# Rotation tables of a state space mixer: two groups side by side in the partitions, laid out for each group by SBUF transfers

## The chip, the cores and the metric

The kernel runs on one core of a Trainium2 chip. The metric is the device time of one execution in microseconds. A core has five engines with instruction streams of their own: TensorE (PE in the rows), VectorE (DVE), ScalarE (ACT), GpSimd (POOL) and SyncE (SP), which in this kernel issues the transfers (DMA). Each engine works through its stream strictly in order, so an instruction that waits holds up all that stand behind it.

## The reference

One decoder layer with two mixers side by side. A normalised input is projected to q, k, v and u. Windowed attention runs over q, k, v; u goes through a diagonal complex state space model with 32 channel groups of 16 channels and 64 states each.

```python
def ssm_mixer(u, h0_re, h0_im, a_re, a_im, log_dt, b_re, b_im, c_re, c_im, d_skip, w_glu, b_glu):
    lr, li, bbr, bbi = zoh_discretize(a_re, a_im, log_dt, b_re, b_im)
    xr = jnp.einsum('blgh,gph->blgp', uf, bbr)
    xi = jnp.einsum('blgh,gph->blgp', uf, bbi)
    ...
    _, _, hr, hi = lax.associative_scan(_ssm_combine, (ar, ai, xr, xi), axis=1)
    y = (jnp.einsum('blgp,ghp->blgh', hr, c_re.astype(f32))
         - jnp.einsum('blgp,ghp->blgh', hi, c_im.astype(f32))
         + d_skip.astype(f32) * uf)
    g = jax.nn.gelu(y)
    ...
```

Each state is multiplied by the same complex number lambda = |lambda| e^(i theta) at every step. Behind the mixers come an output projection with a residual and a SwiGLU feed-forward network. All of it is float32.

## The kernel before

The program has stages: the projection to u together with the parameters of the state space model (`phase_u`, `phase_prep`, about the first 133 us), the mixers (`phase_mix`, to about 556 us), the output projection and the feed-forward network (to the end).

**The state space model.** 2064 prompt tokens are taken in 258 chunks of 8 (`NPC`; with the sample tokens 266, `NC`). For each group TensorE makes the chunk's input to the state, `px <- u, mi`. VectorE turns it into a rotating frame: `xt` and `xs` are `px` times cosine and sine of the angle 8 c theta of chunk c. In that frame the recurrence is real, so one scan on VectorE (`gg`) runs over all chunks. VectorE turns the result back (`xt`, `xs` again, then `hc`), and TensorE makes the outputs `yp <- u, it` and adds `yp <- hc, mo` in the same bank. A group's 64 states fill the 128 partitions twice: real parts in one half, imaginary parts in the other. The rotation of a state's two halves is by the same angle.

**The tables.** `co` and `si` hold these cosines and sines for four groups at a time, as tiles of 128 x 4 x 258, for m = 0 to 7. `ssm_tab1` computes on VectorE the angles in turns, reduced to half a turn on either side: `y` is the angle rounded to whole turns (a multiplication by `ph` and the addition of MAGIC), `f` what is left, from `phh` and `phl`, the angle of 8 theta in two parts. `ssm_tab2` makes the sines on ScalarE: `si` from f, with a scale of either sign in the two halves of the partitions (`s2p`), and `co` from the absolute value of f. As both halves of the partitions have the same angle, each is computed twice. `f` and `y` have one buffer (pool `m_f`), `co` and `si` two (`m_cs`).

**The order of the work.** No instruction is issued where the code stands. All calls go to a `Plan`, which notes them with the tiles that they read and write, and then issues them in the order of a list schedule: of the instructions whose inputs are ready by its own estimates, the one with the longest remaining path goes first. So an edit in one place can move instructions of other stages. All instructions of a trace carry the line of the helper that issues them (L263 before, L279 after); they are told apart by their tiles. The mixers' work is noted by `mix_step`, which interleaves attention tiles with the model's groups; `tab(...)` in it notes the pieces of `ssm_tab1` of a later m.

**Names in the rows.** `pu` are the products of the projection to u, `us` that result in SBUF, `uD` its place in DRAM, from which `u` is read back, laid out for the chunks. `pa` are the products of the projection to q, k, v; `qn` is q normalised, `pt` its transposition on TensorE, `qT` and `kT` the transposed q and k, `ps` the scores, `P` the softmax. `mo`, `t1` are the output matrices of four groups, `mi`, `it`, `gl` matrices that are loaded. The trace's rows leave out all numbers in names, so that `t1` is `t` there.

Of the kernel before, what the change touches and what calls it, by code (L numbers as in the profile page):

```python
# [8 lines left out]
F32 = mybir.dt.float32  # L9
# [8 lines left out]
NP_ = 2064            # prompt tokens with the meta tokens  # L18
TOK = 2128            # and the sample tokens
NT = 17  # L20
NC = TOK // 8         # chunks of 8 tokens
NPC = NP_ // 8
T0 = 16               # the meta tokens go no further than the mixers
TC, TS = 352, 704     # tokens of a chunk and of a block of the last phases
# [5 lines left out]
# columns of the constant array  # L30
# [26 lines left out]
class Lazy:  # L57
    """a view of a tile that is yet to be allocated"""
# [29 lines left out]
    def region(self):  # L88
        return {0} if self.base.psum else set(np.unique(self.idx[::self.base.step]).tolist())
# [80 lines left out]
class Plan:  # L170
    """Stands in for nc: notes the instructions, then issues them in the order of a list schedule
    (longest remaining path first) that keeps every dependency."""
# [9 lines left out]
    def dram(self, shape, dtype, name, blocks):  # L182
        """a scratch array; dependencies are kept by the numbers of its blocks"""
        t = LazyTile(self.bank, [1, 1], dtype, {"name": name})
        t.got, t.psum, t.step = self.dp.tile(list(shape), dtype, name=name), False, 1
        t.count = 1
        return Lazy(t, np.broadcast_to(blocks, shape), (), dtype)

    def turn(self, old, *new):
        """pools that take the place of old ones, once all that was noted on those is through"""  # L190
# [27 lines left out]
    def note(self, eng, name, args, kw):  # L218
# [10 lines left out]
        for t, r, w in use:  # L229
# [11 lines left out]
            for n, rr in t.writes + (t.reads if w else []):  # L241
                if n not in deps and not rr.isdisjoint(r):
                    deps.add(n)
        for t, r, w in use:
            t.first = o.n if t.first is None else t.first
            (t.writes if w else t.reads).append((o.n, r))
            t.pool.ops.add(o.n)
# [41 lines left out]
    def ported(self, eng, name, outs, args, kw):  # L289
        """whether it uses the pair of ports to SBUF that VectorE and GpSimd share"""  # L290
# [9 lines left out]
    def price(self, eng, name, args, kw):  # L300
        """nanoseconds on its engine, and until what follows a transfer may start"""
# [23 lines left out]
    def issue(self):  # L325
# [14 lines left out]
        # a bank is given out once all that its matrix products read has been scheduled  # L340
# [12 lines left out]
        # one that an engine writes for products to be added to it takes a bank that the last product wrote all of  # L353
# [59 lines left out]
class K:  # L413
# [9 lines left out]
    def split_w(self, h, l, raw, g):  # L423
        """h + l = g * raw, both parts exact in float32r"""
# [15 lines left out]
    # ------------------------------------------------------------------ set up  # L440
# [41 lines left out]
    # ------------------------------------------------------------------ u = rms(x) W_u  # L482
    def phase_u(self):
# [12 lines left out]
        for b, n in enumerate((384, 384, 384, 384, 256, 336)):  # L496
# [26 lines left out]
            # 1 / rms of the tokens, in both orientations  # L523
# [26 lines left out]
    # ------------------------------------------------------------------ S5 parameters  # L550
    def phase_prep(self):
# [18 lines left out]
        self.ph, self.phh, self.phl = (pp.tile([128, 32], F32, name=n) for n in ("ph", "phh", "phl"))  # L570
# [4 lines left out]
        self.s2p = pp.tile([128, 1], F32, name="s2p")  # L575
        nc.vector.tensor_scalar(self.s2p, self.sg, TWO_PI, None, op0=ALU.mult)
# [4 lines left out]
        if True:  # L581
# [48 lines left out]
            # theta / 2 pi in turns, as a sum of two floats  # L630
# [19 lines left out]
            nc.vector.tensor_add(self.ph, b8, e8)  # L650
            e8 = add(sub(b8, self.ph), e8)
            hh = cut(self.ph)
            nc.vector.tensor_copy(self.phh, hh)
            nc.vector.tensor_add(self.phl, sub(self.ph, hh), e8)
            # lambda^n, n = 0..8
# [22 lines left out]
            # f = (lambda - 1) / Lambda  # L678
# [20 lines left out]
            # lambda^8 h0  # L699
# [5 lines left out]
            # zero rows of the Toeplitz scratch  # L705
# [3 lines left out]
            # E[(ri p), g, j, h] = lambda^(7-j) B: the taps and, transposed, the chunk input map  # L709
            Ks = t32(shape=(128, 32, 16))  # L710
            # lambda^(7-j)
# [32 lines left out]
    # ------------------------------------------------------------------ S5 mixer  # L744
# [5 lines left out]
    def ssm_mats(self, m):  # L750
        """inputs and matrices of the four groups 4m.."""
# [37 lines left out]
    def ssm_tab1(self, m, piece):  # L789
        """rotations by multiples of 8 theta: the angles in turns"""  # L790
        nc, tp = self.nc, self.m_t
        ix = self.cst[:, C_IX:C_IX + NPC]
        if piece == 0:
            self.m_f = [self.m_fp.tile([128, 4, NPC], F32, name=nm) for nm in "fy"]
        f, y = self.m_f
        if piece == 0:
            for g in range(4):
                nc.vector.tensor_scalar(y[:, g], ix, self.ph[:, 4 * m + g:4 * m + g + 1], MAGIC,
# [3 lines left out]
        elif piece < 6:  # L802
            g = piece - 2
            q = slice(4 * m + g, 4 * m + g + 1)
            nc.vector.scalar_tensor_tensor(f[:, g], ix, self.phh[:, q], y[:, g], op0=ALU.mult, op1=ALU.subtract)
            nc.vector.scalar_tensor_tensor(f[:, g], ix, self.phl[:, q], f[:, g], op0=ALU.mult, op1=ALU.add)
# [4 lines left out]
    def ssm_tab2(self, m):  # L811
        nc, (f, y) = self.nc, self.m_f
        co, si = self.m_st[m][5:7]
        nc.scalar.activation(si, f, AF.Sin, scale=self.s2p)
        nc.scalar.activation(f, f, AF.Abs)
        nc.scalar.activation(co, f, AF.Sin, scale=-TWO_PI, bias=self.hp2)
# [940 lines left out]
```

## Time and profile before

| what | us |
|---|---|
| time, median of three runs | 2153.76 |
| lowest and highest | 2153.35, 2155.02 |
| span of the profiled execution | 2151.2 |
| TensorE busy | 2092.8 (97% of the span) |
| VectorE busy | 1730.0 (80%) |
| ScalarE busy | 1361.0 (63%) |
| GpSimd busy | 88.5 (4%) |

The profile is of one execution, whose span is from the first to the last instruction. Busy time is summed for each engine by itself; an engine that is not busy may be waiting or have nothing to do. The granted clock (PEclk) is TensorE's, as a share of its full speed.

### The profile page before, as it was taken

The page shows a single profiled execution, that of the slowest core. Times are in us where ns is not written, and L with a number is a line of the kernel's source. Part 1 is how long each engine was busy: PE and PEld are TensorE (multiplying, and loading weights), DVE is VectorE, ACT ScalarE, POOL GpSimd, SP SyncE. Part 2 cuts the span into 40 slices and gives each one's busy share as a digit, 9 for nine tenths or more (in the row PEclk, how much of TensorE's full clock was granted, in tenths as well). Part 3 has the DMA queues.
Part 4 walks back from the last instruction along what each step waited for, and adds up shares of the span by engine and source line. Part 5 has one row for each costly group of instructions (what it writes and reads, how often), then busy time and mean ns, then how long its engine had stood idle before and what let it go on. Part 6 is the DMA issues. An engine that isn't in the chain of part 4 may idle for free.

```text
span 2151.2 us, 35211 instructions
## 1 busy us (share of the span) xinstructions
PE 2092.8 (97%) x12557; PEld 1969.8 (92%) x12557; DVE 1730.0 (80%) x3773; ACT 1361.0 (63%) x3001; POOL 88.5 (4%) x80
## 2 busy tenths in 40 slices
PE   7999999999999999999999999999999999999998
PEld 7987777776898999999999999999999999999998
DVE  8889899875488769888787898877878987877876
ACT  6437888878544437566566757656656775665665
POOL 2011011101011000000000000000000000000000
PEclk9999999999899999999999999999999999999999
DMA  6682232214343545323322543332323722222222
GB/s 225 168 171 63 67 94 75 64 53 122 96 122 98 179 152 175 103 74 106 106 79 79 174 160 112 106 98 84 109 69 103 242 83 89 79 69 87 80 71 87
DMA packets 195152, 235.06 MB, mean 109 GB/s; under 512 B 54000, under 2 KB 155792, under 8 KB 194832
## 3 DMA queue, kind: packets, MB, share of 16 engines
q1 hardware_dynamic: 194976, 232.81, 35.4%
q8 instruction: 99, 1.62, 0.3%
q14 instruction: 77, 0.63, 0.1%
HBM read 187.92 MB, written 45.83 MB: 109 GB/s over the span
## 4 chain that ended last, share of the span: by engine, by line
PE 87%; DVE 8%; ACT 2%; DMA 2%; issue 1%; POOL 0%; DVEq 0%; ACTq 0%; POOLq 0%; SPq 0%
PE ga L263 24%; PE gc L263 12%; PE db L263 11%; PE da L263 8%; PE po L263 7%; PE pa L263 6%; PE gb L263 6%; PE ps L263 6%; PE pu L263 2%; PE pt L263 2%; PE px L263 1%; PE yp L263 1%; ACT wb L263 1%; DVE xs L263 1%; DVE acc L263 1%
## 5 line engine op out<-in xcount | busy, mean ns | idle before, releaser
L263 PE MATMUL ga<-X,wb 128*128 128x352 f32 x3168 | 723.2, 324 | 7.0 <-ACT acc L263 2.9
L263 PEld LDWEIGHTS ga<-X,wb 128*128 128x128 f32 x3168 | 544.7, 188 | 10.8 <-ACT gb L263 3.8
L263 PE MATMUL gc<-X,wb 128*128 128x352 f32 x1584 | 403.4, 324 | 1.4 <-ACT acc L263 1.4
L263 ACT ACTIVATE wb<-S 128x512 fp32r<-128x512 f32 (+1 forms) x306 | 187.5, 617 | 155.2 <-PE ga L263 74.6
L263 PEld LDWEIGHTS gc<-X,wb 128*128 128x128 f32 x1584 | 279.6, 188 | 2.1 <-ACT acc L263 2.0
L263 DVE TENSOR_TENSOR wb<-S,wb 128x512 fp32r<-128x512 f32 (+1 forms) x306 | 203.8, 672 | 57.5 <-ACT wb L263 26.9
L263 ACT ACTIVATE wb<-r 128x512 fp32r<-128x512 f32 (+1 forms) x242 | 146.9, 613 | 127.2 <-PE gc L263 47.5
L263 PE MATMUL gb<-X,wb 128*128 128x352 f32 x792 | 217.5, 323 | 0.0
L263 PE MATMUL da<-wb 128*128 128x352 f32 x936 | 208.9, 323 | 3.2 <-DVE acc L263 1.6
L263 DVE TENSOR_TENSOR wb<-r,wb 128x512 fp32r<-128x512 f32 (+1 forms) x242 | 160.2, 670 | 54.8 <-PE gb L263 24.2
L263 PE MATMUL db<-wb 128*128 128x352 f32 x792 | 162.9, 323 | 4.5 <-ACT db L263 4.5
L263 PEld LDWEIGHTS da<-wb 128*128 128x128 f32 x936 | 159.6, 188 | 5.3 <-ACT wb L263 4.6
L263 ACT ACTIVATE wb<-fr 128x512 fp32r<-128x512 f32 (+1 forms) x166 | 101.9, 619 | 93.7 <-PE gc L263 40.7
L263 PE MATMUL db<-gb,wb 128*128 128x352 f32 x792 | 161.1, 323 | 0.0
L263 PE MATMUL pa<-wb,xh 128*128 128x512 f32 (+3 forms) x544 | 156.2, 372 | 0.0
L263 DVE TENSOR_TENSOR wb<-fr,wb 128x512 fp32r<-128x512 f32 (+1 forms) x166 | 111.0, 675 | 41.0 <-PE gb L263 16.9
L263 PEld LDWEIGHTS gb<-X,wb 128*128 128x128 f32 x792 | 142.6, 188 | 0.0
L263 PEld LDWEIGHTS db<-wb 128*128 128x128 f32 x792 | 132.8, 188 | 6.0 <-ACT db L263 6.0
L263 PEld LDWEIGHTS db<-gb,wb 128*128 128x128 f32 x792 | 133.0, 188 | 0.3 <-ACT db L263 0.3
L263 ACT ACTIVATE acc<-db 128x352 f32<-128x352 f32 x288 | 119.4, 457 | 20.6 <-PE db L263 19.9
L263 PE MATMUL po<-oh,wb 128*128 128x352 f32 x576 | 121.3, 334 | 1.8 <-ACT oh L263 1.1
L263 ACT ACTIVATE db<-acc 128x352 f32<-128x352 f32 x276 | 120.4, 465 | 2.4 <-DVE ru L263 2.2
(252 smaller groups left out, 3885.8 us busy)
## 6 DMA issues: line engine op xcount, KB each, us to landing
r<-w_up SPq DMA_DIRECT2D x41, 512.0 KB
r<-w_gate SPq DMA_DIRECT2D x38, 512.0 KB
r<-w_down SPq DMA_DIRECT2D x34, 512.0 KB
fr<-w_gate SPq DMA_DIRECT2D x28, 512.0 KB
fr<-w_down SPq DMA_DIRECT2D x26, 512.0 KB
fr<-w_up SPq DMA_DIRECT2D x25, 512.0 KB
acc<-xT SPq DMA_DIRECT2D x6, 1408.0 KB
hD<-acc SPq DMA_DIRECT2D x6, 1408.0 KB
```

The source lines that it names most:

```text
L263: getattr(getattr(self.nc, eng), name)(*[f(v) for v in args], **{k: f(v) for k, v in kw.items()})
```

## The change

`phase_prep` now lays out the angles for two groups side by side: the even group of a pair in the first 64 partitions, the odd one in the other 64, so that `ph`, `phh`, `phl` have 16 columns in place of 32. `ssm_tab1` computes `f` and `y` as 128 x 2 x 258. `ssm_tab2` makes on ScalarE the sine with both signs (`sp`, `sn`), the absolute value and the cosine (into `y`), all 128 x 2 x 258. Then eight transfers for each m, each from one half of the partitions to a half of `si` or `co`, give every group its table in both halves. They are issued by SP, with the other transfers. `sp` and `sn` are in the pool of `f` and `y`, with one buffer. `mix_step` notes fewer pieces. The rest of the diff changes how `Plan` keeps track of dependencies (sets of numbers become bit masks, and entries that a later write covers are dropped), and takes comments out.

```diff
@@ phase_prep
-        self.ph, self.phh, self.phl = (pp.tile([128, 32], F32, name=n) for n in ("ph", "phh", "phl"))
+        self.ph, self.phh, self.phl = (pp.tile([128, 16], F32, name=n) for n in ("ph", "phh", "phl"))
...
-        self.s2p = pp.tile([128, 1], F32, name="s2p")
-        nc.vector.tensor_scalar(self.s2p, self.sg, TWO_PI, None, op0=ALU.mult)
...
-            nc.vector.tensor_add(self.ph, b8, e8)
-            e8 = add(sub(b8, self.ph), e8)
-            hh = cut(self.ph)
-            nc.vector.tensor_copy(self.phh, hh)
-            nc.vector.tensor_add(self.phl, sub(self.ph, hh), e8)
+            ph = add(b8, e8)
+            e8 = add(sub(b8, ph), e8)
+            hh = cut(ph)
+            pl = add(sub(ph, hh), e8)
+            for y, x in ((self.ph, ph), (self.phh, hh), (self.phl, pl)):
+                for a in range(2):
+                    r = slice(64 * a, 64 * a + 64)
+                    nc.vector.tensor_copy(y[r], x[r].rearrange("p (g a) -> p g a", a=2)[:, :, a])
@@ ssm_tab1
-            self.m_f = [self.m_fp.tile([128, 4, NPC], F32, name=nm) for nm in "fy"]
-        f, y = self.m_f
+            self.m_f = [self.m_fp.tile([128, 2, NPC], F32, name=nm) for nm in ("f", "y", "sp", "sn")]
+        f, y = self.m_f[:2]
         if piece == 0:
-            for g in range(4):
-                nc.vector.tensor_scalar(y[:, g], ix, self.ph[:, 4 * m + g:4 * m + g + 1], MAGIC,
+            for e in range(2):
+                nc.vector.tensor_scalar(y[:, e], ix, self.ph[:, 2 * m + e:2 * m + e + 1], MAGIC,
                                         op0=ALU.mult, op1=ALU.add)
...
-        elif piece < 6:
-            g = piece - 2
-            q = slice(4 * m + g, 4 * m + g + 1)
-            nc.vector.scalar_tensor_tensor(f[:, g], ix, self.phh[:, q], y[:, g], op0=ALU.mult, op1=ALU.subtract)
-            nc.vector.scalar_tensor_tensor(f[:, g], ix, self.phl[:, q], f[:, g], op0=ALU.mult, op1=ALU.add)
+        elif piece < 4:
+            e = piece - 2
+            q = slice(2 * m + e, 2 * m + e + 1)
+            nc.vector.scalar_tensor_tensor(f[:, e], ix, self.phh[:, q], y[:, e], op0=ALU.mult, op1=ALU.subtract)
+            nc.vector.scalar_tensor_tensor(f[:, e], ix, self.phl[:, q], f[:, e], op0=ALU.mult, op1=ALU.add)
@@ ssm_tab2
-        nc, (f, y) = self.nc, self.m_f
+        nc, (f, y, sp, sn) = self.nc, self.m_f
         co, si = self.m_st[m][5:7]
-        nc.scalar.activation(si, f, AF.Sin, scale=self.s2p)
+        nc.scalar.activation(sp, f, AF.Sin, scale=TWO_PI)
+        nc.scalar.activation(sn, f, AF.Sin, scale=-TWO_PI)
         nc.scalar.activation(f, f, AF.Abs)
-        nc.scalar.activation(co, f, AF.Sin, scale=-TWO_PI, bias=self.hp2)
+        nc.scalar.activation(y, f, AF.Sin, scale=-TWO_PI, bias=self.hp2)
+        for out, parts in ((si, (sn, sp)), (co, (y, y))):
+            o = out.rearrange("p (e a) c -> p e a c", a=2)
+            for d in range(2):
+                for a in range(2):
+                    nc.sync.dma_start(o[64 * d:64 * d + 64, :, a], parts[d][64 * a:64 * a + 64])
@@ mix_step
-        tab(2)
+        tab(2, 3)
...
-        tab(3)
...
-        tab(5, 6)
```

The order changes on every engine from the projection to u to the first part of the output projection; the feed-forward network's order is the same. Three places follow, all in the mixer's opening. The numbers behind the names tell buffers apart.

SP, the transfers from the last part of `us` to the first tables' matrices; first before, then after:

```order
L263 DMA uD_75<-us_1393 1024x1x74
L263 DMA r_1472<-xT 128x8x128
L263 DMA r_1491<-xT 128x8x128
L263 DMA uD_75<-us_1393 1024x1x74 x3
L263 DMA mi_1627<-miD_78 128x4x128
L263 DMA u_1639<-uD_75 128x1x266 x2
L263 DMA it_1655<-kD_77 16x4x128 x4
```

```order
L279 DMA uD_75<-us_1393 1024x1x74
L279 DMA si_1536<-sn_1512 64x2x258 x2
L279 DMA uD_75<-us_1393 1024x1x74 x3
L279 DMA co_1579<-y_1437 64x2x258
L279 DMA si_1536<-sp_1506 64x2x258 x2
L279 DMA mi_1621<-miD_78 128x4x128
L279 DMA u_1633<-uD_75 128x1x266 x2
L279 DMA co_1579<-y_1437 64x2x258 x3
L279 DMA it_1661<-kD_77 16x4x128 x4
```


Two `si` transfers now stand ahead of the last three `uD`, and three more ahead of `mi` and `u`; the last three of `co` come behind `u`.

TensorE, from the last `pa` of one attention tile on; before, then after:

```order
L263 MATMUL pa_1665<-wb_449,xl_1466 128x256
L263 MATMUL pt_1759<-idt_199,qn_1752 128x128 x4
L263 MATMUL pa_1769<-wb_449,xh_1602 128x512 x2
L263 MATMUL pa_1769<-wb_449,xl_1681 128x512
...
L263 MATMUL pa_1769<-wb_449,xh_1602 128x512
L263 MATMUL yp_1785<-u_1639,it_1655 128x266
L263 MATMUL yp_1789<-u_1639,it_1655 128x266
L263 MATMUL yp_1785<-hc_1625,mo_1653 128x266
...
L263 MATMUL pt_1798<-idt_199,qn_1752 128x128
```

```order
L279 MATMUL pa_1655<-wb_447,xl_1478 128x256
L279 MATMUL yp_1740<-u_1633,it_1661 128x266
...
L279 MATMUL yp_1740<-hc_1610,mo_1626 128x266
...
L279 MATMUL pt_1775<-idt_199,qn_1768 128x128 x4
L279 MATMUL pa_1786<-wb_447,xh_1629 128x512 x2
L279 MATMUL pa_1786<-wb_447,xl_1651 128x512
...
L279 MATMUL pt_1808<-idt_199,qn_1768 128x128
```


`yp` came behind `pt` and seven `pa` of the next tile; now it comes ahead of both, directly behind the last `pa` of the tile before.

VectorE, the way from `t1` to `hc` of the first two groups; before, then after:

```order
L263 TENSOR_TENSOR f_1563<-f_1563,y_1537 128x1032
L263 TENSOR_TENSOR t1_1642<-ls_114,c2_298 128x512
L263 TENSOR_TENSOR mo_1653<-lr_112,c1_253 128x512
...
L263 TENSOR_TENSOR xl_1681<-r_1414,xh_1602 128x1024
L263 TENSOR_TENSOR xt_1697<-px_1678,co_1552 128x258
...
L263 TENSOR_TENSOR xt_1697<-xt_1697,xs_1703 128x516
...
L263 SCALAR_TENSOR_TENSOR gg_1742<-mag8_1138,xt_1697 128x258 x2
L263 TENSOR_TENSOR qn_1752<-pa_1522,s_1662 128x512
L263 TENSOR_TENSOR xt_1697<-gg_1742,co_1552 128x516
...
L263 TENSOR_TENSOR qn_1752<-pa_1549,s_1662 128x128
L263 TENSOR_TENSOR hc_1625<-xt_1697,xs_1703 128x2x257
```

```order
L279 TENSOR_TENSOR t1_1614<-ls_114,c2_298 128x512
...
L279 TENSOR_TENSOR xl_1651<-r_1416,xh_1629 128x1024
L279 TENSOR_TENSOR mo_1666<-lr_112,c1_253 128x512
L279 TENSOR_TENSOR t1_1676<-ls_114,c2_298 128x512
L279 TENSOR_TENSOR xs_1681<-px_1668,si_1536 64x258
...
L279 TENSOR_TENSOR xt_1686<-xt_1686,xs_1681 128x516
L279 TENSOR_SCALAR y_1721<-cst_203,ph_1074 128x258
L279 SCALAR_TENSOR_TENSOR gg_1725<-mag8_1086,xt_1686 128x258 x2
L279 TENSOR_SCALAR y_1721<-cst_203,ph_1074 128x258
...
L279 TENSOR_TENSOR hc_1610<-xt_1686,xs_1681 128x2x257
L279 TENSOR_SCALAR y_1721<-y_1721 128x516
L279 TENSOR_TENSOR qn_1768<-pa_1528,s_1635 128x512
```


Before, the first row is the end of table m=1 (after, the rows begin at `t1`). Now a second `mo` and `t1` stand ahead of the first `xs`, two `y` of table m=1 stand inside the chain, the rest of that table comes behind `hc`, and `qn` has gone from ahead of `hc` to behind it.

## Rows read from the trace of the kernel before

**Rows 1.** The page: the span, and the busy time of the engines

```profile
span 2151.2 us, 35211 instructions
...
PE 2092.8 (97%) x12557; PEld 1969.8 (92%) x12557; DVE 1730.0 (80%) x3773; ACT 1361.0 (63%) x3001; POOL 88.5 (4%) x80
```

**Rows 2.** By stretch: length, busy PE, PEld, DVE, ACT, POOL, granted clock, DMA share, GB/s

```profile
175.00:500.00 325.00, 322.59 (x1663) 239.19 (x1662) 274.44 (x855) 260.10 (x642) 34.73 (x39) 1.00 0.26 73
```

**Rows 3.** Timeline of TensorE, the mixer's opening: start, length, work, [idle before, releaser]

```profile
153.77 1.12 PE L263 MATMUL pt<-idt,qn 128*128 128x128 f32 x4 [2.21 <-DVE qn L263]
...
157.41 1.06 PE L263 MATMUL yp<-u,it 128*128 128x266 f32 x4
...
158.30 1.06 PE L263 MATMUL yp<-hc,mo 128*128 128x266 f32 x4
```

**Rows 4.** Busy time by stretch: the opening's wait, and what follows it

```profile
150.40:153.80 3.40, 1.19 (x9) 0.90 (x8) 3.36 (x10) 1.97 (x4) 0.00 (x0) 0.98 0.60 166
...
153.80:157.20 3.40, 3.40 (x11) 2.88 (x12) 3.34 (x6) 0.69 (x1) 0.00 (x0) 0.52 0.65 177
```

**Rows 5.** Timeline of TensorE: two waits elsewhere

```profile
53.32 0.43 PE L263 MATMUL pb<-idt,rx 128*128 128x128 f32 x2 [1.69 <-POOL rx L263]
...
547.38 2.80 PE L263 MATMUL pt<-idt,P 16*128 16x16 f32 x12 [3.42 <-ACT P L263]
```

**Rows 6.** Busy time by stretch: behind those waits

```profile
54.60:61.60 7.00, 6.24 (x22) 5.75 (x22) 6.59 (x11) 1.81 (x3) 0.00 (x0) 0.51 0.68 179
...
546.10:559.90 13.80, 12.26 (x56) 11.03 (x57) 9.24 (x22) 11.77 (x33) 0.00 (x0) 0.51 0.05 17
```

**Rows 7.** Groups by line: busy us, mean ns of one, idle before

```profile
L263 DVE TENSOR_SCALAR y<-cst,ph 128x258 f32<-128x258 f32 x32 | 9.9, 349 | 0.3 <-DMA kD<-t 0.3
...
L263 DVE SCALAR_TENSOR_TENSOR f<-cst,phl,f 128x258 f32<-128x258 f32 x32 | 14.4, 480 | 0.0
...
L263 DVE TENSOR_SCALAR y<-y 128x1032 f32<-128x1032 f32 x8 | 5.5, 692 | 0.0
...
L263 DVE TENSOR_TENSOR f<-f,y 128x1032 f32<-128x1032 f32 x8 | 9.8, 1228 | 0.1
...
L263 ACT ACTIVATE si<-f,s2p 128x1032 f32<-128x1032 f32 x8 | 9.3, 1158 | 7.4 <-DVE f L263 7.3
...
L263 ACT ACT_TABLE_LOAD x26 | 33.4, 1283 | 1.2 <-PEq L1747 0.7
```

**Rows 8.** ScalarE around its table load: timeline, then a stretch's busy time

```profile
160.07 1.28 ACT L263 ACT_TABLE_LOAD   x1
...
161.36 0.74 ACT L263 ACTIVATE sq<-sq 128x266 f32<-128x266 f32 x2
...
168.44 0.40 ACT L263 ACTIVATE P<-P,nm 128x128 f32<-128x128 f32 x1 [1.10 <-DVE nm L263]
...
161.40:168.40 7.00, 7.00 (x40) 5.59 (x39) 6.29 (x25) 2.53 (x6) 1.41 (x1) 1.00 0.24 69
```

**Rows 9.** Timeline of VectorE, the mixer's opening

```profile
144.51 0.69 DVE L263 TENSOR_TENSOR t<-ls,c 128x512 f32<-128x512 f32 x1 [1.69 <-DMA uD<-us]
...
145.12 0.69 DVE L263 TENSOR_TENSOR mo<-lr,c 128x512 f32<-128x512 f32 x1
...
148.33 0.41 DVE L263 TENSOR_TENSOR xt<-px,co 128x258 f32<-128x258 f32 x1
...
153.05 0.66 DVE L263 TENSOR_TENSOR qn<-pa,s 128x512 f32<-128x512 f32 x1
...
155.97 0.68 DVE L263 TENSOR_TENSOR hc<-xt,xs 128x514 f32<-128x514 f32 x1
```

**Rows 10.** The chain that ended last: start, length, what

```profile
113.30 6.17 DMA r<-xT
...
135.82 8.50 DMA uD<-us
```

**Rows 11.** Timeline of SP's transfer issues, the mixer's opening

```profile
137.89 1.63 SPq L263 DMA_DIRECT2D u<-uD  x2
```

More of the change, by code (lines that the diff above doesn't have):

```diff
@@ L88, in region @@
     def region(self):
-        return {0} if self.base.psum else set(np.unique(self.idx[::self.base.step]).tolist())
+        if self.base.psum:
+            return 1
+        i = self.idx[::self.base.step]
+        i = i[tuple(slice(0, 1) if s == 0 else slice(None) for s in i.strides)].ravel()
+        bits = np.zeros(int(i.max()) + 1, bool)
+        bits[i] = True
+        return int.from_bytes(np.packbits(bits, bitorder="little").tobytes(), "little")
 def _rearrange(x, pat, n):
@@ L240, in note @@
                 order.add(t.first)
-            for n, rr in t.writes + (t.reads if w else []):
-                if n not in deps and not rr.isdisjoint(r):
+            for n, rr in t.writes:
+                if rr & r:
                     deps.add(n)
+            if w:
+                for n, rr in t.reads:
+                    if rr & r:
+                        deps.add(n)
         for t, r, w in use:
             t.first = o.n if t.first is None else t.first
-            (t.writes if w else t.reads).append((o.n, r))
+            if w:
+                t.writes = [(n, rr) for n, rr in t.writes if rr & ~r]
+                t.reads = [(n, rr) for n, rr in t.reads if rr & ~r]
+                t.writes.append((o.n, r))
+            else:
+                t.reads.append((o.n, r))
             t.pool.ops.add(o.n)
```

## The prediction

> **What bounds the kernel now.** I read the page first: the span is 2151.2 us, and TensorE is busy for 2092.8 us of it, 97% [rows 1]. VectorE comes second with 1730.0 us. The change edits work of VectorE, ScalarE and the transfer queue, all of it in the mixer (about 133 to 556 us), so busy shares over the whole span decide nothing; the next view is the busy time by stretch. From 175 to 500 us TensorE is busy 322.59 of 325.00 us at a granted clock of 1.00, while VectorE has 274.44 [rows 2]. VectorE is heavily used there, but TensorE waits only 2.41 us in all. Whatever VectorE is relieved of in this stretch can return 2.41 us and no more.
>
> The timeline of TensorE then shows where the mixer does wait. One place is its opening: the pa products (the projection to q, k and v) run out and TensorE stands for 2.21 us, from 151.56 until qn comes from VectorE at 153.77 [rows 3]. In the stretch after that wait the granted clock is 0.52, that is the lower of its two levels, with TensorE busy for all 3.40 us [rows 4]. The other is at the mixer's end: 3.42 us for P, a softmax on ScalarE [rows 5], with a clock of 0.51 from 546.1 to 559.9 us behind it [rows 6].
>
> **VectorE's saving.** Per table m (there are eight) the kernel before runs four y<-cst (349 ns), eight multiply-adds (480 ns, as in the row on phl; the four on phh are like it), two passes of 692 ns over 1032 elements and one of 1228 ns [rows 7]. Their busy time is 1.40 + 3.84 + 1.38 + 1.23 = 7.85 us. After, there are two and four of the narrow ones and the wide ones have 516 elements. Halving the last three by width (a lower bound, each has a fixed part) gives 0.70 + 1.92 + 0.69 + 0.61 = 3.92 us. So VectorE is spared some 3.9 us per table, 31 us in all. Nearly all of it lies under a TensorE that does not wait. I take half of the 2.41 us back: **-1.2 us**, bounds -2.4 and 0.
>
> **ScalarE.** Three passes of about 1.1 us (the sine row: 1158 ns [rows 7]) become four over half as many elements: between half the price each (2.3 us) and my value of 0.65 us each, 2.6 us, so the engine is spared under 1 us per table. But the sine needs another function table than tanh and exp, and ScalarE's new order puts six table loads around table m=1, where there was one; in the whole program 30 instead of 26. A load takes 1283 ns [rows 7]. The one in that stretch before starts at 160.07 and the next activation at 161.36 [rows 8], so nothing is added to it. Ahead of the first exp of P, 168.44 before, come four of the loads and two of the sines: 5.1 + 1.3 = 6.4 us of ScalarE. From 161.4 to 168.4 us it was busy for 2.53 of 7.00 us [rows 8], so it has 4.5 us free and the exp could be some 1.9 us late; pt<-P of TensorE comes behind it, with products of the next tile to fill the time. I take **+0.5 us**, bounds 0 and 3.
>
> The Trainium skill, page "ScalarE: Activation LUTs", section "What ACT_TABLE_LOAD costs", gives the same 1283 ns for the load and adds a drain of about 1380 ns to each switch. The row shows no such gap after the load, so here I go by the row. By the page the four loads would cost 10.7 us and not 5.1 us.
>
> **The opening, where the sum is decided.** Before, both first tables are done on VectorE before the stretch begins to press. VectorE then waits until 144.51 for the last uD<-us transfer (the u projection's result on its way to DRAM, whose buffer t1 takes over) [rows 9]; the chain gives that transfer 8.50 us from 135.82 [rows 10]. From there VectorE runs without a gap: t1, mo, the norm, xl, xt at 148.33, qn at 153.05, hc at 155.97 [rows 9]. In the changed order three things move.
>
> First, SP issues two of the new si transfers (132 KB each) ahead of the last three uD<-us. 264 KB at the 166 to 177 GB/s of this stretch [rows 4] are 1.5 us. The transfers may also share the engines and delay nothing, so the bounds are 0 and 1.6. I take 1.5: the chain shows that uD is what VectorE waits for. Five new transfers go ahead of mi and u, of which px is made; an SP issue there takes 0.6 to 0.8 us (two u in 1.63) [rows 11], so u is 3 to 4 us later, and the last three co transfers go behind u. That makes px and co ready at about 150 to 152 us, no earlier than VectorE reaches them. It is the same delay and I count it once.
>
> Second, VectorE gets a second mo and t1 ahead of the first xs and xt: 2 x 0.6 us (t to mo: 144.51 to 145.12) [rows 9]. Table m=1 can't be begun in the idle time before 144.5 any more, since f and y have one buffer and the co transfers read y; two of its y<-cst (0.3 us each) come to stand inside the chain to hc. In return qn and its small sibling (0.66 and about 0.2 us busy) move behind hc. So hc begins at 155.97 + 1.5 + 1.2 + 0.6 - 0.8 = 158.5 and ends at 159.2 us.
>
> Third, TensorE's order now has yp ahead of pt and of the next tile's pa. Before, TensorE did pt and pa from 153.77 to 157.41, at the lower clock, and yp<-hc at 158.30 [rows 3]; that was 3.40 us at 0.52, worth 1.8 us at full clock. After, it has nothing between the last pa and yp<-hc but the two yp<-u (0.4 us), so it stands from 151.6 to about 159.2 us. At that moment it is 0.9 us later than before and has 1.8 us of work still to do, a deficit of 2.7 us. On top comes the clock: 2.21 us of standing were followed by 3.4 us at 0.52 [rows 3, 4], the waits around 53 us by 7.0 us at 0.51 with 6.24 busy, and the 3.42 us by 13.8 us with 12.26 busy [rows 6]. Half of what is done at that level is lost: 1.7, 3.1 or 6.0 us. I take 2.6, somewhat under the middle one, because the first ps must wait a little for kT, now behind a table load, in any case. The opening comes to **+5.3 us**, bounds +2.5 (hc with no transfer delay, the short stretch of low clock) and +9. Behind hc stand qn, the rest of table m=1 and the sq products, so pt and the next ps follow late too; TensorE is full from 160 us on in the kernel before and can't catch up.
>
> **Smaller places.** The planner also reorders the stage from 40 to 60 us, though its work there is nearly the same: VectorE empties one us<-pu bank 37 instructions later, so TensorE loses the pu products that filled the time up to the wait of 1.69 us for rx at 53.32 [rows 5]. By itself that is about 2 us, but the chain waits 6.17 us for a transfer of xT at 113.30 [rows 10], which can swallow it. I take **+0.7**, bounds -1 and +3. At the end the exps stand further ahead on ScalarE: **-0.3**, bounds -6 and +3, with the wait for P [rows 5] and its low clock as what could go. The eight transfers per later table and the 64 issues run on SP beside a full TensorE: 0. The bookkeeping in Lazy and Plan leaves the order as it is: 0.
>
> **Sum.** -1.2 + 0.5 + 5.3 + 0.7 - 0.3 = +5.0 us on the span of 2151.2, 2156.2 us. The median of the timed runs, 2153.76, lies 2.6 us above the profiled span, so the forecast is 2158.8 us. A difference of 0.2% (4.3 us; 2149.45 to 2158.07) is about what a measurement of this kernel can tell from none.
>
> **Rivals.**
> *Relief reaches the end (faster).* If hc is on time, the opening costs +3.5; the steady part gives its 2.4 back; and if the exps moved ahead on ScalarE remove the 3.42 us wait, half of the 12.26 us at 0.51 comes back too, some 3.4 + 4 us. 3.5 - 2.4 - 7.4 is -6.3: 2147.5 us. For it speaks that most of it hangs on a single wait. Against it, that wait is for ScalarE (busy 11.77 of 13.80 us behind it [rows 6]) and not for VectorE, which is what the change spares. It decides once pt<-P at the end starts over 3 us earlier relative to the stage's start. Chance 0.20.
> *All hidden (no change).* The si transfers run beside uD, the px products have u in time, the opening costs +3.0, the steady part gives 2.4 back, the rest cancels: +0.6, 2154.4 us. For it: 31 us less on an engine that is 84% busy, and a sum of small terms of both signs. Against it: TensorE's rows put yp ahead of all work that could fill the wait. Chance 0.33.
> *ScalarE stalls the softmax (slower still).* The sines stand in ScalarE's order ahead of the exps, and f of table m=1 comes from VectorE only behind hc. If ScalarE stands for f, the 4.5 us free [rows 8] are lost and all 6.4 us of loads and sines come on top: the exps are that much late, pt<-P with them, and of the 6.4 us TensorE can fill perhaps 1.4. That is +5 and 2163.8 us. Against it, those two sines need f alone, and the loads themselves wait for nothing. Chance 0.07. (By the drain that the Trainium skill's page "ScalarE: Activation LUTs", section "What ACT_TABLE_LOAD costs", adds to a load, this case would be likelier than that; the trace shows none.)
> The forecast itself, slower by 3 to 8 us, has 0.40.
>
> **Range and chances.** Slower by over 0.2%: 0.40 + 0.07 = 0.47; within: 0.33; faster: 0.20. With bounds of -2.4, 0, +2.5, -1, -6 on one side and 0, +3, +9, +3, +3 on the other, which will not all come together, the range is 2150 to 2165 us; the forecast's own is 2156 to 2162.
>
> **What the profile after would show.** VectorE's busy time down by about 31 us, less if the 516-wide passes cost more than half. In the opening: t1 at about 146 us; yp<-hc at about 159 us, with TensorE standing for over 6 us in one or two pieces since 151 (one before px, if u is late); a granted clock near 0.5 behind it for more than 3.4 us. ScalarE: six loads between 160 and 180 us. The forecast is wrong if yp<-hc comes before 157.5 us, if the clock stays at its upper level there, or if the wait of 3.42 us for P at the mixer's end has gone.

## The result and the profile after

The change makes the kernel slower: 2169.11 us, median of four runs (2164.14 to 2170.19), against 2153.56 of the kernel before on the same chip (2152.74 to 2155.02). The ratio is 1.0071, with an interval of 1.0059 to 1.0083. The profiled execution is the fastest of the four (2164.14 us, span 2162.3); what it shows is some 5 us less than what the median has to explain.

The page, the span and the busy times, answers to [rows 1]:

```profile
span 2162.3 us, 35283 instructions
...
PE 2094.9 (97%) x12557; PEld 1969.2 (91%) x12557; DVE 1707.6 (79%) x3729; ACT 1363.0 (63%) x3013; POOL 91.3 (4%) x80
```

VectorE is relieved, by 22.4 us. The groups by line (busy us, mean ns, idle before) answer to [rows 7]:

```profile
L279 ACT ACT_TABLE_LOAD x30 | 38.5, 1283 | 1.2 <-PEq L1771 0.7
L279 DVE SCALAR_TENSOR_TENSOR f<-cst,phl,f 128x258 f32<-128x258 f32 x16 | 7.1, 480 | 0.0
...
L279 DVE TENSOR_TENSOR f<-f,y 128x516 f32<-128x516 f32 x8 | 5.5, 688 | 0.1
...
L279 DVE TENSOR_SCALAR y<-y 128x516 f32<-128x516 f32 x8 | 3.4, 424 | 0.0
```

The pieces of 258 columns are halved in number at the same price. The wide passes are halved in width, but cost more than half: 424 of 692 ns, 688 of 1228.

The timeline of TensorE, its places ahead of the mixer, in the opening, at the mixer's end and in the feed-forward network:

```profile
49.42 0.90 PE L279 MATMUL pb<-idt,rx 128*128 128x128 f32 x3 [4.07 <-POOL rx L279]
...
148.02 0.69 PE L279 MATMUL px<-u,mi 128*128 128x266 f32 x2 [1.36 <-DMA u<-uD]
149.17 0.72 PE L279 MATMUL px<-u,mi 128*128 128x266 f32 x2 [0.47 <-DMA u<-uD]
...
158.32 1.14 PE L279 MATMUL yp<-hc,mo 128*128 128x266 f32 x4 [1.48 <-issue]
...
196.93 0.52 PE L279 MATMUL pt<-idt,P 128*128 128x128 f32 x3 [3.23 <-DVE su L279]
...
556.48 1.34 PE L279 MATMUL pt<-idt,P 16*128 16x16 f32 x8 [1.14 <-ACT P L279]
558.60 1.36 PE L279 MATMUL pt<-idt,P 16*128 16x16 f32 x4 [0.78 <-ACT P L279]
...
1320.58 5.04 PE L279 MATMUL ga<-X,wb 128*128 128x352 f32 x20 [2.05 <-ACT acc L279]
```

Where [rows 3] have one wait of 2.21 us for qn, there are now two for u and one ahead of `yp <- hc`; and a new one of 3.23 us at 196.93. `su` is the sum of a softmax, added up on VectorE from ScalarE's exps, so that wait is for a softmax. The busy time by stretch (columns as in [rows 2]) shows what follows:

```profile
175.00:500.00 325.00, 317.95 (x1625) 235.53 (x1625) 258.64 (x805) 252.62 (x637) 36.85 (x39) 0.99 0.35 89
...
161.40:168.40 7.00, 7.00 (x36) 5.14 (x35) 6.42 (x23) 5.42 (x9) 3.28 (x1) 1.00 0.56 145
164.90:178.00 13.10, 13.10 (x69) 10.24 (x70) 11.24 (x39) 12.63 (x21) 2.59 (x1) 1.00 0.50 130
...
149.80:153.20 3.40, 3.40 (x14) 3.01 (x13) 2.94 (x10) 0.00 (x0) 0.69 (x1) 0.50 0.71 169
197.60:201.00 3.40, 3.40 (x10) 2.44 (x10) 3.14 (x12) 2.21 (x6) 0.00 (x0) 0.50 0.04 4
1319.00:1325.00 6.00, 4.42 (x18) 4.43 (x19) 4.68 (x10) 4.33 (x12) 0.00 (x0) 0.72 0.28 87
```

In the first line, the stretch in which [rows 2] had TensorE standing for 2.41 us, it now stands for 7.05 us, and behind the wait for su it works for 3.4 us at the lower level of its clock, which loses another 1.7 us: some 6.3 us in a stretch where the prediction had -1.2 and +0.5.

How the exps came late is read from ScalarE's timeline, which answers to [rows 8]:

```profile
164.98 1.28 ACT L279 ACT_TABLE_LOAD   x1
166.28 0.64 ACT L279 ACTIVATE sp<-f 128x516 f32<-128x516 f32 x1
166.93 1.28 ACT L279 ACT_TABLE_LOAD   x1
168.23 0.48 ACT L279 ACTIVATE sq<-px,bg 128x266 f32<-128x266 f32 x1
168.73 1.28 ACT L279 ACT_TABLE_LOAD   x1
170.02 0.63 ACT L279 ACTIVATE sn<-f 128x516 f32<-128x516 f32 x1
170.67 1.28 ACT L279 ACT_TABLE_LOAD   x1
171.97 0.40 ACT L279 ACTIVATE P<-P,nm 128x128 f32<-128x128 f32 x1
...
174.16 1.28 ACT L279 ACT_TABLE_LOAD   x1
175.46 0.73 ACT L279 ACTIVATE y<-f,hp 128x516 f32<-128x516 f32 x1
176.20 1.28 ACT L279 ACT_TABLE_LOAD   x1
177.50 0.21 ACT L279 ACTIVATE ex<-ex 128x4 f32<-128x4 f32 x1
...
180.63 1.27 ACT L279 ACTIVATE P<-P,su 128x128 f32<-128x128 f32 x4
```

and, of the kernel before, the last two of these rows:

```profile
165.11 0.21 ACT L263 ACTIVATE ex<-ex 128x4 f32<-128x4 f32 x1
...
174.06 1.29 ACT L263 ACTIVATE P<-P,su 128x128 f32<-128x128 f32 x4 [1.07 <-DVE su L263]
```

Between two function tables ScalarE goes to and fro for single activations: six loads in 12.5 us. From 164.9 to 178.0 us it is busy for 12.63 of 13.10 us. The first exp of P is at 171.97 instead of 168.44, 3.5 us later. Its input `nm` is ready on VectorE at 169.84 instead of 168.40, so 1.4 us of that come from the opening and 2.1 us from the loads and sines that stand ahead on ScalarE. Behind the exps stand the cosine and two more loads, 3.3 us in all, and only then `ex`, which `su` needs and which before came ahead of the exps. So P is normalised (`P <- P, su`) at 180.63 instead of 174.06, 6.6 us later. TensorE does not stand there; it runs out of other products only at 193.70. The P that it then waits for, of the next softmax, is normalised from 195.79 on. Until 192.55 ScalarE had stood for 4.36 us for an `ex` from VectorE, so the delay does not reach this wait through ScalarE's queue alone, and its way there is not shown step by step.

By the mixer's end `pt <- P` of [rows 5], at 547.38 before, is at 556.48, 9.1 us later, although its own wait fell from 3.42 to 1.14 and 0.78 us. The last 1.5 us of the span's 11.1 come at 1320.58: a wait of 2.05 us that the kernel before has too, but with a mean clock of 0.72 in the six microseconds, where the same place of before (1309.5 to 1315.5) has 1.00. That term is not the change's: the clock is 0.72 there in e12 too, which is no slower than the kernel before, and 1.00 in e1 and e6.

### The profile page after: what moved, and what is told of

It reads as the page before. It is cut to its first block, busy times and chain, and to the rows that moved or that the text cites. A ratio compares the mean times of both kernels' runs of the same rounds, so it can differ in the third digit from the quotient of the medians.

```text
span 2162.3 us, 35283 instructions
## 1 busy us (share of the span) xinstructions
PE 2094.9 (97%) x12557; PEld 1969.2 (91%) x12557; DVE 1707.6 (79%) x3729; ACT 1363.0 (63%) x3013; POOL 91.3 (4%) x80
## 4 chain that ended last, share of the span: by engine, by line
PE 83%; DVE 10%; ACT 2%; DMA 2%; issue 1%; SPq 1%; POOL 0%; DVEq 0%; ACTq 0%
PE ga L279 24%; PE gc L279 12%; PE db L279 11%; PE da L279 8%; PE po L279 7%; PE gb L279 6%; PE ps L279 5%; PE pa L279 5%; PE pu L279 2%; PE pt L279 1%; DVE xs L279 1%; PE yp L279 1%; PE px L279 1%; DVE xt L279 1%; DVE acc L279 1%
## 5 line engine op out<-in xcount | busy, mean ns | idle before, releaser
L279 DVE TENSOR_TENSOR wb<-S,wb 128x512 fp32r<-128x512 f32 (+1 forms) x306 | 203.4, 670 | 59.8 <-ACT wb L279 27.2
L279 PE MATMUL pa<-wb,xh 128*128 128x512 f32 (+3 forms) x544 | 158.3, 376 | 0.0
```

The lines of the kernel that those rows point to most:

```text
L279: getattr(getattr(self.nc, eng), name)(*[f(v) for v in args], **{k: f(v) for k, v in kw.items()})
```

## The experiments

Two theories stood at the start. The first: the loss is made in the mixer's opening by two things, the new transfers on SP that stand ahead of u, and the sines of table m=1, late on ScalarE because the `co` transfers hold y. The rival: the loss is that of the whole new order, which differs on every engine from 40 us on, or of the transfers' traffic all along. Each ratio is against the kernel before on the same chip (medians there 2155.91 to 2157.35 us); the ratios are those on record and differ from the quotients of the medians by up to 0.0009.

| experiment | median us | ratio | interval |
|---|---|---|---|
| e8, the change again | 2170.11 | 1.0059 | 1.0044 to 1.0074 |
| e1, cosine in a tile of its own | 2163.0 | 1.0031 | 1.0017 to 1.0046 |
| e2, a table's activations together | 2162.54 | 1.0038 | 1.0023 to 1.0052 |
| e11, both | 2170.68 | 1.0062 | 1.0049 to 1.0074 |
| e3, before with all transfers | 2160.39 | 1.0025 | 1.0013 to 1.0037 |
| e12, the same for tables 2 to 7 alone | 2155.91 | 0.9995 | 0.9986 to 1.0004 |
| e6, before with VectorE's relief alone | 2156.55 | 1.0003 | 0.9994 to 1.0013 |
| e4, the change in before's order, late transfers | 2160.83 | 1.0018 | 1.0009 to 1.0026 |
| e5, the same, early transfers | 2164.96 | 1.0035 | 1.0021 to 1.0048 |
| e9, before's order, change from table 2 on | 2159.6 | 1.0013 | 1.0004 to 1.0022 |
| e10, planner free, change from table 2 on | 2160.41 | 1.0020 | 1.0011 to 1.0029 |

**e6, the relief alone.** The kernel before in its own order, in which VectorE's passes on the tables have half their columns.

```diff
         if piece == 0:
             for g in range(4):
+                nc.skip = g > 1
...
-            nc.vector.tensor_scalar(y, y, MAGIC, None, op0=ALU.subtract)
+            self.half(v, "tensor_scalar", (y, y, MAGIC, None), (yh, yh, MAGIC, None), op0=ALU.subtract)
```

> The kernel before, in its own order on all engines, with VectorE's work on the tables at half the width (and the absolute value on ScalarE too); the tables of two groups are made from those of the other two, so that part of the computation is left out. Theory A: the relief lies under a full TensorE, 2150 to 2154 us. If VectorE's load sets the mixer's time after all: under 2147.

VectorE's busy time is 1706.3 us, as in the change, and the ratio 1.0003. The relief is worth nothing that can be told from the noise. In the profiled run TensorE is busy 323.00 of the 325 us of [rows 2], where it was 322.59.

**e3 and e12, the transfers alone.** The kernel before with eight transfers per table out of `si` and `co` into an unused array, in an order that is otherwise that of before; in e12 for tables 2 to 7 only.

```diff
+        for i in range(8):
+            x = (si, co)[i // 4].rearrange("p (e a) c -> p e a c", a=2)
+            d, a = i // 2 % 2, i % 2
+            nc.sync.dma_start(self.jD[8 * m + i], x[64 * d:64 * d + 64, :, a])
```

> The kernel before, with eight more transfers per table on SP's queue, of the same size (64 x 2 x 258) and from co and si, but into a DRAM array that nobody reads; the order on all compute engines is that of before. Theory A: the transfers cost little by themselves, 2153 to 2157 us, by a later t1 and hc in the opening. Theory B: most of the loss, 2162 us or more.

> The kernel before with the eight added transfers for tables 2 to 7 only, 48 in place of 64, none of them near the mixer's opening; the order of the four compute engines is that of before. If transfers cost by their place ahead of u in the opening (my theory), the wait of px for u is that of before, the ratio is 1.0000 to 1.0008 and the time at most 1.5 us above the kernel before. If transfers cost by their number (traffic, 132 KB each, all along the mixer), three quarters of the 4 to 5 us that all 64 cost are left: ratio 1.0014 to 1.0020.

All 64 cost 1.0025, between the two theories' ranges; the 48 of the later tables 0.9995. So it isn't the traffic, and the price lies with the 16 of the opening. These transfers go to DRAM and nobody waits for them, so what it costs that `xt` and `xs` wait for tables laid out by transfers is not in these two runs. The timeline of SP in e3, its transfer issues, shows the place:

```profile
135.25 2.51 SPq L263 DMA_DIRECT2D jD<-si  x4
...
138.53 2.72 SPq L263 DMA_DIRECT2D jD<-co  x4
...
142.92 3.30 SPq L263 DMA_DIRECT2D u<-uD  x2
```

The two u are issued 5.0 us later than in [rows 11], and TensorE waits for them:

```profile
152.27 2.16 PE L263 MATMUL px<-u,mi 128*128 128x266 f32 x4 [5.65 <-DMA u<-uD]
```

**e4 and e5, the whole change in the order of before.** Every instruction of the change takes the place of the one that it replaces, with a tile of its own for the cosine. The transfers stand behind the first two u (e4), or directly behind the sines (e5).

```diff
+            for i, o in enumerate(row):
+                for used, do in extra.get(i, ()):
+                    do(self.nc)
...
+                    nc.late.append(((at, self.m_u[m]), use, lambda n, x=x, y=y: n.sync.dma_start(x.real(), y.real())))
```

> The whole change (tables side by side, sines of both signs, cosine in a tile of its own, eight transfers per table), but issued in the order of the kernel before on TensorE, VectorE and ScalarE; SP issues the transfers of a table behind its first two u loads and behind its cosine. If the loss lies in the new order (table m=1 in the softmax, a finer alternation of products on TensorE) and in the place of the transfers on SP, nothing of it is left: 2150 to 2156 us against 2154 to 2156 of before, no wait of px for u over 1 us. If the transfers' traffic costs as such: 2159 or more, as with the transfers alone.

> As the one before, with the transfers of a table on SP as soon as its sines and its cosine are made, ahead of the last uD and of mi and u. If their place on SP is what they cost: 4 to 6 us slower than the late place, with px waiting 3 to 6 us for u at about 147 us. If the traffic as such costs, both are the same.

TensorE's waits over 0.5 us in the opening of e4:

```profile
149.13 0.71 PE L270 MATMUL px<-u,mi 128*128 128x266 f32 x2 [0.72 <-DMA u<-uD]
...
159.72 1.11 PE L270 MATMUL pt<-idt,qn 128*128 128x128 f32 x4 [5.79 <-DVE qn L270]
```

and of e5:

```profile
148.10 1.33 PE L270 MATMUL px<-u,mi 128*128 128x266 f32 x4 [1.17 <-DMA u<-uD]
...
156.83 1.12 PE L270 MATMUL pt<-idt,qn 128*128 128x128 f32 x4 [3.31 <-DVE qn L270]
...
163.91 2.11 PE L270 MATMUL yp<-u,it 128*128 128x266 f32 x4 [2.97 <-DMA it<-kD]
```

With the transfers behind u, VectorE stands for `co` in front of `xt` and qn comes late behind it; with them ahead, it is u and then `it`. Either way some 6.5 to 7.5 us of standing take the place of 2.21 us. Both missed in part: e4 is 5 us above what was expected of it, in the range that was to speak for the traffic (against which e12 speaks), and e5 is 4 us slower than e4, as expected, but px waits 1.17 us and not 3 to 6. Still e4 costs 1.0018 and the change 1.0059 to 1.0071. The work of the change in the old order, with a tile for the cosine, costs about 4 us, or 8 with the transfers early; the rest comes with the lack of that tile or with the planner's order.

**e1, e2 and e11: the sines.** e1 gives the cosine its own tile, so that the `co` transfers no longer hold y. e2 makes the planner issue the four activations of a table one behind the other (18 table loads instead of 30). e11 has both.

```diff
-            self.m_f = [self.m_fp.tile([128, 2, NPC], F32, name=nm) for nm in ("f", "y", "sp", "sn")]
+            self.m_f = [self.m_fp.tile([128, 2, NPC], F32, name=nm) for nm in ("f", "y", "sp", "sn", "cs")]
...
-        nc.scalar.activation(y, f, AF.Sin, scale=-TWO_PI, bias=self.hp2)
+        nc.scalar.activation(cs, f, AF.Sin, scale=-TWO_PI, bias=self.hp2)
```

```diff
+            rows = {e: [o for o in row if o.n in rest] if e == "scalar" and rest else row for e, row in cand.items()}
...
+            if e == "scalar" and not rest and o.n in group:
+                rest = set(group[o.n])
```

> The changed kernel with one edit: the cosine goes into a tile of its own, so that no transfer reads y and table m=1 can be begun while the transfers of m=0 still run. By its order pt stands ahead of yp again and table m=1 is through on ScalarE before the first softmax. Theory A (the loss comes from y being held by the transfers, which pushes table m=1 into the softmax): 2152 to 2158 us, no wait of over 2 us near 193 us. Theory B (the transfers themselves cost: SP's queue and the traffic): 2164 us or more, as the change. Theory C (any new order of this planner costs some us by itself): 2158 to 2166.

> The changed kernel, with the four activations of a table kept together on ScalarE by the planner: for table m=1 two table loads in place of five between tanh and exp, 18 loads in all in place of 30. y is still held by the transfers and yp still stands ahead of pt. Theory A, where the alternation on ScalarE is the larger half of the loss and the late hc the smaller: 2158 to 2164 us, with the opening's loss of about 3 us still there. If the loads cost nothing: 2167 to 2170.

Each gives back some 5 to 9 us of the change's 13 to 16, and in both the wait for su is gone. (e1 and e4 have the same work and a cosine tile: 1.0031 in the planner's order, 1.0018 in that of before, with intervals that overlap.) ScalarE's timeline in e2:

```profile
169.97 1.28 ACT L279 ACT_TABLE_LOAD   x1
171.26 0.64 ACT L279 ACTIVATE sp<-f 128x516 f32<-128x516 f32 x1
...
173.13 0.73 ACT L279 ACTIVATE y<-f,hp 128x516 f32<-128x516 f32 x1
173.88 1.28 ACT L279 ACT_TABLE_LOAD   x1
```

e2 is where its theory A put it. e1 is not: 2163.0 is above the 2152 to 2158 of its theory A, and in the range of its theory C, by which a new order of the planner's costs some us by itself. The pages show where. e6 and e1 ran on the same chip, with spans of 2155.0 and 2163.2 us; first e6, then e1:

```profile
PE 2092.3 (97%) x12557; PEld 1969.5 (91%) x12557; DVE 1706.3 (79%) x3725; ACT 1360.3 (63%) x3001; POOL 87.8 (4%) x80
PE 2100.7 (97%) x12557; PEld 1975.0 (91%) x12557; DVE 1709.2 (79%) x3729; ACT 1364.5 (63%) x3011; POOL 88.7 (4%) x80
```

TensorE stands equally long in both (span less busy time, 62.7 and 62.5 us) and is busy 8.4 us longer in e1 for the same 12557 products. So e1's loss is no wait at all. In the seven profiled executions of the old order TensorE is busy for 2092.3 to 2095.9 us, in the six of the planner's new orders for 2094.9 (the change) to 2100.7.

e11 was to show whether the two edits mend one delay or two.

> The change with both edits: the cosine in a tile of its own, and the four activations of a table kept together in ScalarE's order. If the two edits mend the same delay of the softmax (my theory), it stands within 2 us of the better one of them, at about 2161 to 2163 us, ratio 1.0025 to 1.0040, and the wait of TensorE for su near 197 us is absent as it is with either. If they mend two separate delays, their gains of about 7 us each against the change add up, and it stands at 2154 to 2157 us, ratio 1.0015 or less.

It showed a third thing that neither expectation had: 1.0062, as slow as the change and slower than either edit alone. The wait for su is absent, as expected, and TensorE is busy 324.24 of the 325 us from 175 to 500. But its opening now has these waits:

```profile
153.00 2.08 PE L279 MATMUL px<-u,mi 128*128 128x266 f32 x4 [2.61 <-DMA u<-uD]
...
163.19 1.33 PE L279 MATMUL yp<-hc,mo 128*128 128x266 f32 x4 [1.91 <-issue]
...
167.31 1.30 PE L279 MATMUL pt<-idt,qn 128*128 128x128 f32 x5 [2.78 <-DVE qn L279]
```

They sum to 7.3 us; those of the change itself, with the one for su, to 6.5 (1.36, 0.47, 1.48, 3.23), in e8 to 7.4 us (2.27, 0.50, 1.34, 3.24); those of e2 to 4.6 and of e1 to 2.6. Of these five, all in an order of the planner's, those with 6.5 us or more stand at 1.0059 to 1.0071 and the other two at 1.0031 and 1.0038. The wait for su itself goes with the sines between the softmax's parts: from the first scores `ps` to the normalised P it is 17.3 us in the change and in e8, which have the wait, and 8.5, 12.4, 13.2 and 13.5 us in e1, e2, e11 and the kernel before, which don't. But that curing it is by itself worth 7 us has fallen. I read it so that the late softmax is how this order pays for a crowded opening, and another order pays at u, hc and qn; five orders don't prove it.

**e8, e9 and e10.** e8 is the change a second time, on another chip. e9 and e10 leave tables 0 and 1, those of the opening, as they were, and apply the change from m=2 on: e9 in the order of before, e10 with the planner free.

```diff
-        f, y = self.m_f[:2]
+        w = 4 if m < 2 else 2
+        f, y = (x[:, 0:w] for x in self.m_f)
...
+        if m < 2:
+            nc.scalar.activation(si, f, AF.Sin, scale=self.s2p)
...
+            return
```

> The change as it is, on the same chip and beside the same runs of before as the other two: 13 to 17 us over before. Its trace shows how much of the difference between the profiled 2164 and the median of 2169 us lies ahead of the mixer: 2 to 5 us there if the waits for rx and us near 48 and 120 us vary, none if it is elsewhere.

> Tables m=0 and m=1 made as in the kernel before, without transfers; the change (side by side, transfers) from m=2 on; the order of the kernel before on TensorE. If the 3.6 us that were left with the old order and the late transfers all lie in the opening: 0 to 1 us over before, within 0.1%. If transfers or moved work cost in the later tables too: 2 to 4 us over before.

> The same division of the tables, but the planner orders the work freely, with y holding the cosine as in the change. If the planner turns VectorE's relief into time once the opening is out of the way: 2 us or more under before. If a new order costs by itself what it alternates more finely: 2 to 6 us over before. If neither: within 2 us.

e8 repeats the result, and the wait for su with it (3.24 us, at 203.11). Its profiled execution answers the question put to it: the last product of the projection to u starts at 137.55, in the change's profile at 133.86, so 3.7 us of the 6.4 by which its span is longer lie ahead of the mixer. With the first two tables left as they were, the planner's order keeps TensorE's opening as it was, and the loss falls from about 14 us to 4.3 us (1.0020). Its one long wait there is that of [rows 3], for qn, now 2.39 us. Two thirds of the loss belong to tables 0 and 1. Both fell where their expectations had a cost left, of the later tables (e9) or of the order (e10). What remains in e9 and e10 (some 3 to 4 us, lower bounds of 0.9 and 2.4) isn't any one wait that the traces show, and is open. In e10 it is no standing: by the pages TensorE stands 59.8 us, 2.4 less than in e9, and is busy 5.1 us more (2098.8 against 2093.7). The runs of the relief alone (e6) and of the later transfers alone (e12) show none of it; the one more sine pass per table, with the wait of `xs` and `xt` for a transfer in place of an activation, was not tried by itself.

Not tried: the new order without its transfers, and the change with two buffers for f and y.

## Why the prediction was wrong

The direction was right, but the time is 10 us above the forecast and 4 us above the range.

**VectorE's saving (-1.2): worth nothing.** The time spared was estimated at 31 us "less if the 516-wide passes cost more than half", and they do. That it can return no more than TensorE's 2.41 us of standing was the right reading of [rows 2]; e6 shows no gain (0.9994 to 1.0013).

**ScalarE (+0.5, bounds 0 and 3): the step that failed.** The prediction counted four loads and two sines as 6.4 us against 4.5 us of free time and left 1.9 us, of which TensorE would fill most. For what it counted, that was right: the first exp comes 2.1 us behind its input. But the sum stopped at the first exp. The other two of its six loads and the cosine, 3.3 us behind the exps and ahead of `ex`, it put at nothing, and the softmax isn't done before `ex` is. P is normalised 6.6 us late, 1.4 of it from the opening; TensorE fills the time at that softmax, as said, but at the next one it stands for 3.23 us and loses 1.7 us more by its clock: about +5 against bounds of 0 and 3.

The rival in which ScalarE waits for f, set at 0.07, had this number, in part by luck. Its premise was right: "f of table m=1 comes from VectorE only behind hc" (the last pass on f is at 163.30). But ScalarE didn't stand for f; its one wait in that stretch is 1.51 us for px, and of the 4.5 us free it used 2.9 (5.42 of 7.00 us busy). The rival's 5 us were standing alone; the 1.7 us by the clock were not in it.

The Trainium skill, "ScalarE: Activation LUTs", section "What ACT_TABLE_LOAD costs", would add a drain of about 1380 ns to each switch. The trace disagrees once more: load at 164.98, next activation at 166.28, 1.30 us from one start to the other. The loads cost what their row says; there were too many of them in one place.

**The opening (+5.3, bounds +2.5 and +9): the right mechanism, sized too high for the profiled run.** VectorE's timeline there answers to [rows 9]:

```profile
144.78 0.69 DVE L279 TENSOR_TENSOR t<-ls,c 128x512 f32<-128x512 f32 x1 [8.84 <-DMA uD<-us]
...
150.66 0.43 DVE L279 TENSOR_TENSOR xt<-px,co 128x258 f32<-128x258 f32 x1 [0.31 <-DMA co<-y]
...
157.53 0.69 DVE L279 TENSOR_TENSOR hc<-xt,xs 128x514 f32<-128x514 f32 x1
```

`t1` is at 144.78, not 146: the two `si` transfers delay uD by 0.3 us where 1.5 were taken. hc is at 157.53 (158.5 in the sum) and `yp <- hc` at 158.32 (159.2). VectorE stands for 8.84 us ahead of `t1`, where it stood for 1.69 us: that is the time in which table m=1 had been made, and the reason that its f comes late to ScalarE. TensorE's wait has parted in three, the first for u, as said; but the lower clock fell on the `pa` products at 149.8 to 153.2, 3.40 us as in [rows 4], and not behind `yp`, so no more was lost to it than before. From 158.3 to 163.3 us the clock is 1.00; that is one of the signs by which the prediction was to be wrong. TensorE stood for 3.3 us there and not for over 6, since u and the lower clock put its `pa` later. The first scores `ps` start at 163.31, before at 160.56: +2.8 us. "It is the same delay", said of u, co and uD, held in this execution; e3 shows the price of u's place alone where nothing else is late: 5.65 us.

**40 to 60 us (+0.7, bounds -1 and +3): mis-sized.** The wait for rx is 4.07 us at 49.42 and not 1.69. In this one execution it is made up again by 133 us, as the prediction thought it could be; the other traces in which the planner orders the whole change (e1, e2, e8, e11) have waits of 3.4 to 4.1 us for rx too, and start the last product of the projection to u at 136.0 to 138.5 us, the traces with the old order at 133.7 to 135.6. (e10, whose first two tables are those of before, has 1.68 and 134.6.) That makes about +2 to +3, and the profiled run was a lucky one there. In e8, a profile near the median on another chip, it is 3.7 of the 6.4 us by which the span is longer; the place was not tried by itself.

**The mixer's end (-0.3).** The wait for P is 1.92 us instead of 3.42, so part of what the rival of "relief" wanted did come, but TensorE arrives there 9 us late and keeps that.

**The order itself (no term).** That the planner's orders keep TensorE busy longer for the same products, 8.4 us in e1 against e6, had no term in the prediction, which asked of the new order only where TensorE would stand. What makes it so is open.

The sum by the profiled run (span +11.1): relief 0; opening +2.8; the late softmax about +5; spread over the rest of the mixer about +2; the feed-forward network's clock +1.5, which runs of either order have or lack. These say where the time went in that execution. They are not what each place would give back: e11 has the second at nothing and is as slow. The range was too narrow because the bounds of ScalarE's term took in a late first exp, but not the loads behind it, and because it had nothing for the order itself.

## What to carry to other kernels

A saving on an engine that isn't waited for is worth at most the bound engine's idle time, and here it was worth nothing; the price of an edit is where its new transfers and waits stand, so cost it in the one crowded place and not as an average. Ask of work that slides late not only how long it takes, but which idle time it has missed: VectorE's idle time ahead of the opening had held a whole table. Follow a softmax to its last part, not to its first exp. And where a list scheduler sets the order, time the same work in the old order too: here it cost 4 to 8 us there, by the place of its transfers, and 7 to 15 in the planner's orders, and two edits that each won 5 to 9 us won nothing together. Look at the bound engine's busy time as well as at its waits.

## What the runs showed of the hardware that was not expected

- 48 transfers of 132 KB from SBUF to DRAM cost nothing beside a full TensorE (0.9995 in e12), though the DMA share from 175 to 500 us goes from 0.26 to 0.35; eight of them on SP ahead of the small loads of u make TensorE stand for 5.65 us (e3).
- The same 544 products `pa <- wb,xh` of the mixer are longer busy in another order, without a gap in which TensorE stands. In the groups by line from 134 to 556 us it has, in the change and then in e1, where the kernel before had 156.2 us and 372 ns:

```profile
L279 PE MATMUL pa<-wb,xh 128*128 128x512 f32 (+3 forms) x544 | 158.3, 376 | 0.0
```

```profile
L279 PE MATMUL pa<-wb,xh 128*128 128x512 f32 (+3 forms) x544 | 161.2, 378 | 0.0
```

The products overlap in time, and a group's busy time counts what it shares with products of another kind too, so not all of these 2.1 and 5.0 us are lost; the page's busy time, which counts each moment once, is 2092.8, 2094.9 and 2100.7 us. That it comes of a finer mixing of kinds of products was seen in the orders only, and not tried.
- The clock's lower level came for 3.4 us behind waits of 1.36 with 0.47 us, and for 3.4 us behind one of 3.23 us. Behind the wait of 2.05 us in the feed-forward network, whose order the change leaves as it is, the mean clock of six microseconds is 0.72 in the change, e8, e9, e11 and e12, and 1.00 in the kernel before, e1 and e6.
